# Gate and up projections: three of eight weight tiles with seven products, their shared sums written into the accumulators first

## The chip, the cores and the metric

The kernel runs on one core of a Trainium2 chip. The metric is the device time of one execution in microseconds (us). The work is shared by TensorE (PE, matrix products), ScalarE (ACT, copies and activations), VectorE (DVE, elementwise work), GpSimd (POOL, hardly used here) and SyncE (SP), which issues the loads from HBM. Each engine works off its own list of instructions in the order written in that list; an instruction whose input isn't ready, or whose output buffer isn't free yet, holds up everything behind it on its engine.

## The reference

One layer of a hybrid encoder on 256 positions with model width 2048: a projection of the normalised input, three mixers, an output projection, and a SwiGLU block. The change lies in the first half of the SwiGLU block alone:

```
h = rmsnorm(x, ffn_norm_g)                         # 256 x 2048
x = x + (silu(h @ w_gate) * (h @ w_up)) @ w_down   # w_gate, w_up: 2048 x 5632
```

All data are float32. The kernel keeps that accuracy by splitting every operand of a product into a high part (rounded to the narrower format fp32r) and the low rest, and summing three products: high x high, high x low, low x high. So each 128x128x512 block product costs three matmuls, and each weight needs two passes before it can be used: ACT writes the high part (`copy`), then DVE subtracts it from the weight (`subtract`) to get the low part.

## The kernel before

The 5632 columns of gate and up are worked off in 11 groups of 512 columns (`for g in range(11)`, L926). In a group the 2048 rows of the weights are 8 tiles of 256 rows (two blocks of 128), each loaded for gate and for up. A tile of gate and up together with the two blocks of 128 positions is a 2x2 by 2x2 block product, eight block products in all.

**Plain tiles** (`plain_unit`, L899). The eight block products go into four accumulators, PSUM banks of the pool `psA` (4 banks): c11 and c21 are gate for the first and second 128 positions, c12 and c22 are up. Per tile 4 x 2 x 3 = 24 matmuls, and two weight slabs of 128x1024, each with one ACT copy and one DVE subtraction (`halve`, L859). The four buffers for high parts and four for low parts go round.

**Fast tiles** (`fast_weights`, L866; `fast_unit`, L889). For the first `FAST = 2` tiles of a group the 2x2 by 2x2 product is done with seven block products in place of eight (Winograd's form of Strassen's scheme): 21 matmuls. It needs sums of the activations, which are made once (`turn_x2`, L805, into two packed tiles per weight tile), and differences of the weights, T, made for every group on DVE. Four of the products are shared between outputs and are summed in the four banks of the other PSUM pool, `psM` (ACROSS: p1, p6, p7, p5); three belong to one output each (ALONE: c11, c21, c12) and go straight into its accumulator. The differences have high and low parts of their own, in the buffers hT and lT, two of each, one per fast tile.

At the end of the shared products p1 is copied out of its bank by ACT (u1), and DVE makes u2 = p1 + p6, u3 = u2 + p7, u2 + p5 and u3 + p5 (L938 to L942), all held in SBUF. After the last plain tile DVE adds them to the four accumulators, ACT applies Silu, DVE multiplies gate with up (L951 to L955), and TensorE transposes the result (`turn_hid`, L912) among the plain tiles of the next group, into a `psM` bank too.

The order of each engine's list is made by a scheduler that goes through the program and takes, at each step, the instruction of highest priority that is ready by its estimates. Work inside `tc.high_priority(offset=ahead[0])` (loads and splitting of weights) is placed as though it stood 400 instructions earlier.

Of the kernel before, what the change touches and what calls it, by code (L numbers as in the profile page):

```python
# [30 lines left out]
ROWS = {"w_in": 2048, "w_uq": 512, "w_ukv": 256, "w_o": 2048, "w_gate": 2048, "w_up": 2048, "w_down": 5632}  # L31
# [21 lines left out]
SABBUFS = 3  # L53
WARM = 9
RAWS = 4
FAST = 2
MAGIC = 12582912.0
LOGEXP = "natural_log_exp_and_others"

# [1 line left out]
def build(tc, x, xT, pos, gains, fgain, lbraw, w_in, w_uq, w_ukv, w_o, w_gate, w_up, w_down, cst, msk, out, dbg=None):  # L61
    nc = tc.nc
    pe, act, dve, pool, sp = nc.tensor, nc.scalar, nc.vector, nc.gpsimd, nc.sync
# [41 lines left out]
    ahead = [0]  # L105
# [224 lines left out]
    f = rt(0)  # L330
# [464 lines left out]
    def wo_end(a, g):  # L795
        t = x2[g]
        for b in range(2):
            tt(t[:, b, :], t[:, b, :], a[b], ALU.add)
            junk = ffp.tile([P, 512], F32, name=nm("s1"), tag="s1", bufs=1)
            act.activation(junk, t[:, b, :], AF.Square, accum_out=ss2[:, 2 * g + b:2 * g + b + 1])  # L800
        kept = dram.tile([P, 2, 512], F32, name=nm("kept"), tag=f"kept{g}", bufs=1)
        act.dma_start(kept, t)
        x2kept.append(kept)

        def turn_x2():  # L805
            yield
            for i in range(2):
                n = 2 * g + i
                ps = transpose4([[t[:, b, (2 * i + j) * P:(2 * i + j + 1) * P] for b in range(2)] for j in range(2)])
                if n >= FAST:  # L810
                    at = act_tile()
                    for j in range(2):
                        split_act(at, j, ps[:, j * 256:(j + 1) * 256], gc(G_FFN, 2 * n + j))
                    x2T[n] = at
                    continue

                A = ffp.tile([P, 8, P], F32, name=nm("T"), tag="T")
                for j in range(2):
# [12 lines left out]
        spawn(turn_x2())
# [27 lines left out]
    def halve(src, js, hi=None, lo=None):  # L859
        hi = hi or slabp.tile([P, 2, 512], F32R, name=nm("hi"), tag="hi")  # L860
        lo = lo or slabp.tile([P, 2, 512], F32R, name=nm("lo"), tag="lo")
        act.copy(hi[:, js, :], src[:, js, :])  # L862
        tt(lo[:, js, :], src[:, js, :], hi[:, js, :].bitcast(F32), ALU.subtract)
        return hi, lo

    def fast_weights(wa, wb, r0, c0):  # L866

        with tc.high_priority(offset=ahead[0]):
            W = ffp.tile([P, 4, 512], F32, name=nm("W"), tag="W")
            for w, js in ((wb, slice(0, 2)), (wa, slice(2, 4))):  # L870
                at = ROWS[w.tensor.name] * c0 + r0 * 512
                sp.dma_start(W[:, js, :], w[at:at + 2 * P * 512].rearrange("(p t c) -> p t c", p=P, t=2))
            T = ffp.tile([P, 4, 512], F32, name=nm("T"), tag="T")
            tt(T[:, 0:2, :], W[:, 0:1, :].broadcast_to([P, 2, 512]), W[:, 1:3, :], ALU.subtract)
            tt(T[:, 2, :], W[:, 1, :], T[:, 1, :], ALU.subtract)
            tt(T[:, 3, :], W[:, 3, :], T[:, 2, :], ALU.subtract)
            hT = ffp.tile([P, 4, 512], F32R, name=nm("hT"), tag="hT")
            lT = ffp.tile([P, 4, 512], F32R, name=nm("lT"), tag="lT")
            a = halve(W[:, 2:4, :], slice(0, 2))
            halve(T, slice(0, 2), hT, lT)  # L880
            halve(T, slice(2, 4), hT, lT)
            b = halve(W[:, 0:2, :], slice(1, 2))
        return a, b, (hT, lT)


    ACROSS = (("p1", 0, 0, 0), ("p6", 5, 2, 2), ("p7", 6, 2, 0), ("p5", 4, 2, 1))
    ALONE = (("c11", 2, 0, 1), ("c21", 3, 2, 3), ("c12", 7, 1, 1))

    def fast_unit(accs, products, ws, forms, start):  # L889
        ah, al = forms  # L890
        for name, f, which, k in products:
            hi, lo = ws[which]
            o = accs[name]
            last = name[0] == "p" and start == "last"
            pe.matmul(o, lhsT=ah[:, f, :], rhs=hi[:, k, :], start=start is True, stop=False)  # L895
            pe.matmul(o, lhsT=ah[:, f, :], rhs=lo[:, k, :], start=False, stop=False)  # L896
            pe.matmul(o, lhsT=al[:, f, :], rhs=hi[:, k, :], start=False, stop=last)  # L897

    def plain_unit(accs, wa, wb, at, start, stop):  # L899
        for nme, b, (hi, lo) in (("c11", 0, wa), ("c21", 1, wa), ("c12", 0, wb), ("c22", 1, wb)):  # L900
            o = accs[nme]
            for j in range(2):
                ah = at[:, 0, j, b * P:(b + 1) * P]
                al = at[:, 1, j, b * P:(b + 1) * P]
                pe.matmul(o, lhsT=ah, rhs=hi[:, j, :], start=start and nme == "c22" and j == 0, stop=False)  # L905
                pe.matmul(o, lhsT=ah, rhs=lo[:, j, :], start=False, stop=False)  # L906
                pe.matmul(o, lhsT=al, rhs=hi[:, j, :], start=False, stop=stop and j == 1)  # L907

    def part(tag, bufs=1):
        return ffp.tile([P, 512], F32, name=nm(tag), tag=tag, bufs=bufs)  # L910
# [15 lines left out]
    for g in range(11):  # L926
        accs = {}
        fast = [fast_weights(w_gate, w_up, i * 256, g * 512) for i in range(FAST)]
        for n in ("p1", "p6", "p7", "p5"):
            accs[n] = bank()  # L930
        for i in range(FAST):
            fast_unit(accs, ACROSS, fast[i], x2T[i], True if i == 0 else "last" if i == FAST - 1 else False)
        for n in ("c11", "c21", "c12", "c22"):
            accs[n] = acc1()
        for i in range(FAST):
            fast_unit(accs, ALONE, fast[i], x2T[i], i == 0)
        u1, u3, u2, u4 = part("s1"), part("u3"), part("u2", 2), part("v", 2)
        act.copy(u1, accs["p1"])  # L938
        tt(u2, u1, accs["p6"], ALU.add)
        tt(u3, u2, accs["p7"], ALU.add)  # L940
        tt(u2, u2, accs["p5"], ALU.add)
        tt(u4, u3, accs["p5"], ALU.add)  # L942
        for i in range(FAST, 8):
            with tc.high_priority(offset=ahead[0]):
                wa = halve(load(w_gate, i * 256, g * 512), slice(0, 2))
                wb = halve(load(w_up, i * 256, g * 512), slice(0, 2))
            plain_unit(accs, wa, wb, x2T[i], i == FAST, i == 7)
            if g == 0 and i == FAST:
                flush()
            tick()  # L950
        for b, (ug, cg, uu, cu) in enumerate(((u1, "c11", u2, "c12"), (u3, "c21", u4, "c22"))):  # L951
            tt(ug, ug, accs[cg], ALU.add)
            act.activation(ug, ug, AF.Silu, scale=r2[:, b:b + 1])
            tt(uu, uu, accs[cu], ALU.add)
            stt(uu, uu, r2[:, b:b + 1], ug, ALU.mult, ALU.mult)  # L955
        spawn(turn_hid(g, (u2, u4)))

    hid = {}
    pairs = []
# [138 lines left out]
```

## Time and profile before

| | |
|---|---|
| median of 3 runs | 1132.84 us (1132.2 to 1132.9) |
| the profiled execution's own time | 1133.12 us |
| its span, first to last instruction | 1131.4 us |
| busy of the span: PE, DVE, ACT | 99%, 67%, 53% |
| granted TensorE clock over the span | 0.998 |
| gate and up, first matmul to the last group | 404 to about 880 us |
| one group in the steady state | 43.28 us, DVE busy for 33.40, ACT for 22.25 |

The busy share of an engine tells how much of the time something was in flight on it. The period of a group is read from the start of a group's first shared matmul to that of the next. A wait in the trace stands behind the instruction that waited, in brackets, with the engine and line that released it.

### The profile page before, as it was taken

The page shows a single profiled execution, that of the slowest core. Times are in us where ns is not written, and L with a number is a line of the kernel's source. Part 1 is how long each engine was busy: PE and PEld are TensorE (multiplying, and loading weights), DVE is VectorE, ACT ScalarE, POOL GpSimd, SP SyncE. Part 2 cuts the span into 40 slices and gives each one's busy share as a digit, 9 for nine tenths or more (in the row PEclk, how much of TensorE's full clock was granted, in tenths as well). Part 3 has the DMA queues.
Part 4 walks back from the last instruction along what each step waited for, and adds up shares of the span by engine and source line. Part 5 has one row for each costly group of instructions (what it writes and reads, how often), then busy time and mean ns, then how long its engine had stood idle before and what let it go on. Part 6 is the DMA issues. An engine that isn't in the chain of part 4 may idle for free.

```text
span 1131.4 us, 14321 instructions
## 1 busy us (share of the span) xinstructions
PE 1117.2 (99%) x5363; PEld 941.7 (83%) x5363; DVE 758.4 (67%) x907; ACT 595.2 (53%) x791; POOL 76.4 (7%) x110
## 2 busy tenths in 40 slices
PE   8999999999999999999999999999999999999997
PEld 5888899999988888888888888888888888888886
DVE  7798555455557876886886877876967645454543
ACT  7665565556545654554554555544546534443433
POOL 3196000010100000000000000000000000000000
PEclk9999999999999999999999999999999999999999
DMA  7745465544676765655656656556638666666662
GB/s 263 244 147 167 119 181 180 155 131 144 208 252 205 222 207 185 205 191 184 208 191 194 203 171 213 196 169 206 201 117 287 212 198 191 188 193 195 189 198 98
DMA packets 73302, 215.18 MB, mean 190 GB/s; under 512 B 7440, under 2 KB 24592, under 8 KB 73232
## 3 DMA queue, kind: packets, MB, share of 16 engines
q1 hardware_dynamic: 72656, 212.16, 58.8%
q10 hardware_dynamic: 576, 2.10, 0.5%
q8 instruction: 42, 0.69, 0.2%
q14 instruction: 28, 0.23, 0.1%
HBM read 210.04 MB, written 4.19 MB: 189 GB/s over the span
## 4 chain that ended last, share of the span: by engine, by line
PE 93%; DMA 2%; DVE 2%; issue 2%; ACT 1%; SPq 0%; POOL 0%; ACTq 0%; POOLq 0%; DVEq 0%
PE acc L153 15%; PE acc L155 15%; PE acc L154 15%; PE acc L906 10%; PE acc L907 10%; PE acc L905 10%; PE bank L248 2%; PE bank L895 2%; PE bank L896 2%; PE bank L897 2%; PE acc L895 1%; PE acc L896 1%; PE acc L897 1%; DVE lo L93 1%; PE bank L712 1%
## 5 line engine op out<-in xcount | busy, mean ns | idle before, releaser
L93 DVE TENSOR_TENSOR lo<-raw,hi 128x1024 fp32r<-128x1024 f32 (+3 forms) x366 | 424.3, 1167 | 279.3 <-ACT hi L121 217.7
L121 ACT CAST hi<-raw 128x1024 fp32r<-128x1024 f32 (+3 forms) x234 | 223.0, 956 | 246.2 <-PE acc L155 224.2
L154 PE MATMUL acc<-lo,at 128*128 128x512 f32 (+2 forms) x808 | 302.4, 374 | 3.1 <-DVE lo L93 2.9
L153 PE MATMUL acc<-hi,at 128*128 128x512 f32 (+2 forms) x808 | 304.4, 379 | 0.0
L155 PE MATMUL acc<-hi,at 128*128 128x512 f32 (+2 forms) x808 | 301.3, 373 | 0.0
L905 PE MATMUL acc<-hi,at 128*128 128x512 f32 x528 | 207.5, 393 | 0.0
L906 PE MATMUL acc<-lo,at 128*128 128x512 f32 x528 | 205.6, 389 | 0.3 <-DVE lo L93 0.3
L907 PE MATMUL acc<-hi,at 128*128 128x512 f32 x528 | 205.7, 390 | 0.0
L862 ACT CAST hi<-raw 128x1024 fp32r<-128x1024 f32 x132 | 136.6, 1051 | 130.0 <-PE acc L907 97.2
L154 PEld LDWEIGHTS acc<-lo,at 128*128 128x128 f32 x808 | 152.0, 188 | 29.3 <-DVE lo L93 7.6
L153 PEld LDWEIGHTS acc<-hi,at 128*128 128x128 f32 x808 | 151.7, 188 | 24.0 <-ACT hi L121 1.3
L155 PEld LDWEIGHTS acc<-hi,at 128*128 128x128 f32 x808 | 151.9, 188 | 22.1
L906 PEld LDWEIGHTS acc<-lo,at 128*128 128x128 f32 x528 | 99.2, 188 | 21.0 <-DVE lo L93 1.1
L907 PEld LDWEIGHTS acc<-hi,at 128*128 128x128 f32 x528 | 99.1, 188 | 20.8
L905 PEld LDWEIGHTS acc<-hi,at 128*128 128x128 f32 x528 | 99.2, 188 | 19.8
L177 POOL TENSOR_TENSOR sm<-sm,expo 128x4 f32<-128x4 f32 (+2 forms) x14 | 12.0, 858 | 896.8 <-DVE sm L102 896.8
L93 DVE TENSOR_TENSOR lo<-W,hi 128x1024 fp32r<-128x1024 f32 (+1 forms) x44 | 42.0, 956 | 34.6 <-ACT hi L862 34.6
L862 ACT CAST hi<-W 128x1024 fp32r<-128x1024 f32 (+1 forms) x44 | 36.7, 834 | 49.8 <-PE acc L907 42.7
L93 DVE TENSOR_TENSOR lT<-T,hT 128x1024 fp32r<-128x1024 f32 x44 | 52.6, 1216 | 0.0
L862 ACT CAST hT<-T 128x1024 fp32r<-128x1024 f32 x44 | 45.1, 1046 | 0.5 <-DVE T L93 0.4
L93 DVE TENSOR_TENSOR T<-W,T 128x512 f32<-128x512 f32 x44 | 30.0, 683 | 0.1
L93 DVE TENSOR_TENSOR T<-W 128x1024 f32<-128x1024 f32 x22 | 26.8, 1220 | 1.8 <-DMA W<-w_gate 1.6
(252 smaller groups left out, 1096.2 us busy)
## 6 DMA issues: line engine op xcount, KB each, us to landing
raw<-w_down SPq DMA_DIRECT2D x88, 512.0 KB, 4.2
raw<-w_gate SPq DMA_DIRECT2D x66, 512.0 KB, 4.1
raw<-w_up SPq DMA_DIRECT2D x66, 512.0 KB, 4.4
raw<-w_in SPq DMA_DIRECT2D x48, 384.0 KB, 3.5
raw<-w_in SPq DMA_DIRECT2D x32, 512.0 KB, 3.5
raw<-w_o SPq DMA_DIRECT2D x32, 512.0 KB, 4.3
W<-w_up SPq DMA_DIRECT2D x22, 512.0 KB, 3.6
W<-w_gate SPq DMA_DIRECT2D x22, 512.0 KB, 4.6
```

Of the source, the lines that this page charges most:

```text
L93: dve.tensor_tensor(o, a, b, op=op)
L121: act.copy(hi[:, js, :n], raw[:, js, :n])
L153: pe.matmul(o, lhsT=ah, rhs=hi[:, j, cs], start=start and j == 0, stop=False)
L154: pe.matmul(o, lhsT=ah, rhs=lo[:, j, cs], start=False, stop=False)
L155: pe.matmul(o, lhsT=al, rhs=hi[:, j, cs], start=False, stop=stop and j == 1)
L862: act.copy(hi[:, js, :], src[:, js, :])
L895: pe.matmul(o, lhsT=ah[:, f, :], rhs=hi[:, k, :], start=start is True, stop=False)
L896: pe.matmul(o, lhsT=ah[:, f, :], rhs=lo[:, k, :], start=False, stop=False)
L897: pe.matmul(o, lhsT=al[:, f, :], rhs=hi[:, k, :], start=False, stop=last)
L905: pe.matmul(o, lhsT=ah, rhs=hi[:, j, :], start=start and nme == "c22" and j == 0, stop=False)
L906: pe.matmul(o, lhsT=ah, rhs=lo[:, j, :], start=False, stop=False)
L907: pe.matmul(o, lhsT=al, rhs=hi[:, j, :], start=False, stop=stop and j == 1)
```

## The change

`FAST` goes from 2 to 3: per group a third tile with 21 matmuls, and five plain tiles in place of six. The weight tiles W get 3 buffers (2 before), T gets one (2 before); hT and lT keep two each. `fast_weights` now makes only the split parts of the four shared products, all in hT and lT; the three parts for the products of one output are split later by `alone_weights`, for the third tile into the same hT and lT buffers. So a group writes four pairs (hT, lT) into two buffers, where it was two pairs.

The sums are no longer added at the end. ACT copies p1 into c11's bank, u3 into c21's bank, DVE writes u2 + p5 and u3 + p5 into c12's and c22's banks, and only then do the matmuls of these accumulators start, adding to what stands there (no matmul of them has the start flag). The four adds behind the last plain tile are gone.

```diff
-FAST = 2
+FAST = 3
...
     def fast_weights(wa, wb, r0, c0):
         with tc.high_priority(offset=ahead[0]):
-            W = ffp.tile([P, 4, 512], F32, name=nm("W"), tag="W")
-            for w, js in ((wb, slice(0, 2)), (wa, slice(2, 4))):
-                at = ROWS[w.tensor.name] * c0 + r0 * 512
-                sp.dma_start(W[:, js, :], w[at:at + 2 * P * 512].rearrange("(p t c) -> p t c", p=P, t=2))
-            T = ffp.tile([P, 4, 512], F32, name=nm("T"), tag="T")
-            tt(T[:, 0:2, :], W[:, 0:1, :].broadcast_to([P, 2, 512]), W[:, 1:3, :], ALU.subtract)
+            W = ffp.tile([P, 4, 512], F32, name=nm("W"), tag="W", bufs=3)
...
+            sp.dma_start(W[:, 0:2, :], vb)
+            sp.dma_start(W[:, 3, :], va[:, 0, :])
+            sp.dma_start(W[:, 2, :], va[:, 1, :])
+            T = ffp.tile([P, 3, 512], F32, name=nm("T"), tag="T", bufs=1)
+            tt(T[:, 0:2, :], W[:, 0:1, :].broadcast_to([P, 2, 512]), W[:, 1:4:2, :], ALU.subtract)
             tt(T[:, 2, :], W[:, 1, :], T[:, 1, :], ALU.subtract)
-            tt(T[:, 3, :], W[:, 3, :], T[:, 2, :], ALU.subtract)
-            hT = ffp.tile([P, 4, 512], F32R, name=nm("hT"), tag="hT")
-            lT = ffp.tile([P, 4, 512], F32R, name=nm("lT"), tag="lT")
-            a = halve(W[:, 2:4, :], slice(0, 2))
-            halve(T, slice(0, 2), hT, lT)
-            halve(T, slice(2, 4), hT, lT)
-            b = halve(W[:, 0:2, :], slice(1, 2))
-        return a, b, (hT, lT)
+            tt(W[:, 0, :], W[:, 2, :], T[:, 2, :], ALU.subtract)
+            hT, lT = wide("hT"), wide("lT")
+            split(hT[:, 0:3, :], lT[:, 0:3, :], T)
+            split(hT[:, 3, :], lT[:, 3, :], W[:, 3, :])
+        return W, (hT, lT)
...
+    def split(hi, lo, src):
+        act.copy(hi, src)
+        tt(lo, src, hi.bitcast(F32), ALU.subtract)
+
+    def alone_weights(W, last):
+        with tc.high_priority(offset=ahead[0]):
+            if last:
+                hT, lT = wide("hT"), wide("lT")
+                split(hT[:, 0:3, :], lT[:, 0:3, :], W[:, 0:3, :])
+                return [(hT[:, k, :], lT[:, k, :]) for k in range(3)]
+            h1, l1 = halve(W[:, 0:2, :], slice(0, 2))
+            h2, l2 = halve(W[:, 2:4, :], slice(0, 1))
+        return [(h1[:, 0, :], l1[:, 0, :]), (h1[:, 1, :], l1[:, 1, :]), (h2[:, 0, :], l2[:, 0, :])]
...
+        for n in ("p1", "p6", "p7", "p5"):
+            across(n, 0)
+        for i in range(1, FAST):
+            for n in ("p1", "p6", "p7"):
+                across(n, i)
+        for i in range(1, FAST):
+            across("p5", i)
+        rest = [alone_weights(fast[i][0], i == FAST - 1) for i in range(FAST)]
         for n in ("c11", "c21", "c12", "c22"):
             accs[n] = acc1()
-        for i in range(FAST):
-            fast_unit(accs, ALONE, fast[i], x2T[i], i == 0)
-        u1, u3, u2, u4 = part("s1"), part("u3"), part("u2", 2), part("v", 2)
+        u1, u2, u3 = part("s1"), part("u2"), part("u3")
         act.copy(u1, accs["p1"])
+        act.copy(accs["c11"], u1)
         tt(u2, u1, accs["p6"], ALU.add)
         tt(u3, u2, accs["p7"], ALU.add)
-        tt(u2, u2, accs["p5"], ALU.add)
-        tt(u4, u3, accs["p5"], ALU.add)
+        act.copy(accs["c21"], u3)
+        tt(accs["c12"], u2, accs["p5"], ALU.add)
+        tt(accs["c22"], u3, accs["p5"], ALU.add)
+        for n in ("c11", "c21", "c12"):
+            for i in range(FAST - 1):
+                alone(n, i, rest[i])
+        for n in ("c11", "c21", "c12"):
+            alone(n, FAST - 1, rest[FAST - 1])
...
-        for b, (ug, cg, uu, cu) in enumerate(((u1, "c11", u2, "c12"), (u3, "c21", u4, "c22"))):
-            tt(ug, ug, accs[cg], ALU.add)
-            act.activation(ug, ug, AF.Silu, scale=r2[:, b:b + 1])
-            tt(uu, uu, accs[cu], ALU.add)
-            stt(uu, uu, r2[:, b:b + 1], ug, ALU.mult, ALU.mult)
-        spawn(turn_hid(g, (u2, u4)))
+        hh = []
+        for b, (cg, cu) in enumerate((("c11", "c12"), ("c21", "c22"))):
+            sg, v = part("sg", 2), part("v", 2)
+            act.activation(sg, accs[cg], AF.Silu, scale=r2[:, b:b + 1])
+            stt(v, accs[cu], r2[:, b:b + 1], sg, ALU.mult, ALU.mult)
+            hh.append(v)
+        spawn(turn_hid(g, hh))
```

How the lists of the engines change is shown at three places, for a group in the middle. The names: u_1088 and u_1089 (u_1069 and u_1068 before) are u2 and u3, s_... is u1, banks 5292 to 5295 are p1, p6, p7, p5 of this group, 5636 to 5638 are p1, p6, p7 of the next group, 5472 takes transposes of the group before; acc_5352, acc_5353, acc_5354 and acc_5355 are c11, c21, c12 and c22.

The first place is DVE at the start of a group. Before, u2 and u3 stand behind the first tile's differences and ahead of all the rest:

```order
L93 TENSOR_TENSOR T_5561<-W_5558 128x1024
L96 SCALAR_TENSOR_TENSOR u_1002_4976<-u_1002_4976,sm_3859,s_1000_4974 128x512
L93 TENSOR_TENSOR T_5561<-W_5558,T_5561 128x512
L96 SCALAR_TENSOR_TENSOR v_4977<-v_4977,sm_3859,u_1001_4975 128x512
L93 TENSOR_TENSOR T_5561<-W_5558,T_5561 128x512
L93 TENSOR_TENSOR u_1069_5314<-s_1067_5312,bank_5263 128x512
L93 TENSOR_TENSOR u_1068_5313<-u_1069_5314,bank_5264 128x512
L93 TENSOR_TENSOR T_5582<-W_5579 128x1024
```

Now, in the list after the change, DVE has this behind the low parts of the third tile's shared products (lT_5287, whose last row is the first here):

```order
L93 TENSOR_TENSOR lT_5287<-W_5278,hT_5286 128x512
L93 TENSOR_TENSOR T_5598<-W_5594 128x1024
L93 TENSOR_TENSOR lT_5349<-W_5278,hT_5348 128x1536
L93 TENSOR_TENSOR T_5598<-W_5594,T_5598 128x512
L93 TENSOR_TENSOR lT_5603<-W_5594,hT_5602 128x512
L93 TENSOR_TENSOR W_5594<-W_5594,T_5598 128x512
L93 TENSOR_TENSOR lo_5396<-raw_5393,hi_5395 128x1024
L93 TENSOR_TENSOR lo_5402<-raw_5399,hi_5401 128x1024
L93 TENSOR_TENSOR lT_5603<-T_5598,hT_5602 128x1536
L93 TENSOR_TENSOR u_1088_5357<-s_1087_5356,bank_5293 128x512
L93 TENSOR_TENSOR T_5612<-W_5608 128x1024
L93 TENSOR_TENSOR u_1089_5358<-u_1088_5357,bank_5294 128x512
```

T_5598 and lT_5603 belong to the next group's first tile, T_5612 to its second, lo_5396 and lo_5402 to this group's first plain tile. u2 has moved from the sixth row to behind all of them.

The second place is PE behind the products of one output. Before, the last of these products was followed by the first plain tile at once:

```order
L895 MATMUL acc_4954<-hi_4920,at_3477 128x512
L896 MATMUL acc_4954<-lo_4921,at_3477 128x512
L897 MATMUL acc_4954<-hi_4920,at_3478 128x512
L905 MATMUL acc_4952<-hi_4985,at_3550 128x512
L906 MATMUL acc_4952<-lo_4986,at_3550 128x512
L907 MATMUL acc_4952<-hi_4985,at_3550 128x512
```

Now, after the change, PE has done the nine products of c11 and one plain matmul when it comes to this:

```order
L917 MATMUL acc_5352<-lo_5396,at_3566 128x512
L917 MATMUL acc_5352<-hi_5395,at_3566 128x512 x2
L917 MATMUL acc_5352<-lo_5396,at_3566 128x512
L917 MATMUL acc_5352<-hi_5395,at_3566 128x512
L908 MATMUL bank_5636<-hT_5602,at_3461 128x512
L908 MATMUL bank_5636<-lT_5603,at_3461 128x512
L908 MATMUL bank_5636<-hT_5602,at_3462 128x512
L908 MATMUL bank_5637<-hT_5602,at_3461 128x512
L908 MATMUL bank_5637<-lT_5603,at_3461 128x512
L908 MATMUL bank_5637<-hT_5602,at_3462 128x512
L908 MATMUL bank_5638<-hT_5602,at_3461 128x512
L908 MATMUL bank_5638<-lT_5603,at_3461 128x512
```

Three shared products of the next group's first tile (9 matmuls; its p5 stays behind the last plain tile) have moved in ahead of c21's products, which follow two rows on.

The third place is ACT around the copy of p1. Before, the copy stood alone between a high part for the second tile's c12 product and the first plain slab:

```order
L862 CAST hi_5258<-W_5241 128x512
L938 COPY s_1067_5312<-bank_5262 128x512
L862 CAST hi_5323<-raw_5321 128x1024
L862 CAST hT_5565<-T_5561 128x1024
L862 CAST hi_5329<-raw_5327 128x1024
```

Now three wide copies into the hT buffers come ahead of it:

```order
L862 CAST hi_5344<-W_5264 128x512
L888 CAST hT_5286<-T_5282 128x1536
L888 CAST hT_5286<-W_5278 128x512
L888 CAST hT_5348<-W_5278 128x1536
L963 COPY s_1087_5356<-bank_5292 128x512
L964 COPY acc_5352<-s_1087_5356 128x512
L888 CAST hT_5602<-W_5594 128x512
L931 COPY at_5429<-bank_5430 128x512
L862 CAST hi_5395<-raw_5393 128x1024
L862 CAST hi_5401<-raw_5399 128x1024
L888 CAST hT_5602<-T_5598 128x1536
```

hT_5286 is the third tile's shared part and takes the buffer that the first tile had; hT_5348 is the third tile's part for its own three products and takes the second tile's; hT_5602 is the next group's.

## Rows read from the trace of the kernel before

**Rows 1.** The page: busy us, share and instructions; the chain that ended last, by engine.

```profile
PE 1117.2 (99%) x5363; PEld 941.7 (83%) x5363; DVE 758.4 (67%) x907; ACT 595.2 (53%) x791; POOL 76.4 (7%) x110
...
PE 93%; DMA 2%; DVE 2%; issue 2%; ACT 1%; SPq 0%; POOL 0%; ACTq 0%; POOLq 0%; DVEq 0%
```

**Rows 2.** Stretch of one group: us, busy us per engine (instructions), PEclk, DMA share, GB/s.

```profile
534.37:577.65 43.28, 43.28 (x196) 35.70 (x194) 33.40 (x37) 22.25 (x25) 0.00 (x0) 1.00 0.60 196
```

**Rows 3.** The waits of PE: engine, line, releaser, us in total, times, longest.

```profile
PE acc L154 <- DVE lo L93: 2.9, 6, 0.8
```

**Rows 4.** PE in order of time: start us, us, line, out<-in.

```profile
578.33 0.40 PE L895 MATMUL bank<-hT,at 128*128 128x512 f32 x1
...
580.20 0.40 PE L897 MATMUL bank<-hT,at 128*128 128x512 f32 x1
...
580.89 0.39 PE L897 MATMUL bank<-hi,at 128*128 128x512 f32 x1
...
587.35 0.39 PE L905 MATMUL acc<-hi,at 128*128 128x512 f32 x1
...
592.57 0.39 PE L907 MATMUL acc<-hi,at 128*128 128x512 f32 x1
...
593.47 0.39 PE L906 MATMUL acc<-lo,at 128*128 128x512 f32 x1
```

**Rows 5.** DVE operations by shape, 404 to 885 us: busy us, mean ns, idle before.

```profile
L93 DVE TENSOR_TENSOR lo<-raw,hi 128x1024 fp32r<-128x1024 f32 x136 | 164.0, 1221 | 63.7 <-ACT hi L862 60.7 <-ACT hi L121 2.4
...
L93 DVE TENSOR_TENSOR T<-W,T 128x512 f32<-128x512 f32 x40 | 27.3, 683 | 0.1
...
L93 DVE TENSOR_TENSOR u<-s,bank 128x512 f32<-128x512 f32 x11 | 7.5, 679 | 1.7 <-PE bank L897 1.7
```

**Rows 6.** ACT operations by shape, 404 to 885 us.

```profile
L862 ACT CAST hi<-raw 128x1024 fp32r<-128x1024 f32 x132 | 136.6, 1051 | 130.0 <-PE acc L907 97.2 <-PE acc L897 21.6 <-DMA raw<-w_up 3.3
...
L862 ACT CAST hi<-W 128x512 fp32r<-128x512 f32 x21 | 13.0, 620 | 27.8 <-PE acc L907 26.1 <-PE acc L155 1.7
...
L938 ACT COPY s<-bank 128x512 f32<-128x512 f32 x11 | 6.5, 587 | 29.7 <-PE bank L897 29.7
```

**Rows 7.** DVE in order of time, 577 to 621 us.

```profile
577.41 0.68 DVE L93 TENSOR_TENSOR u<-u,acc 128x512 f32<-128x512 f32 x1
578.01 0.68 DVE L93 TENSOR_TENSOR v<-v,acc 128x512 f32<-128x512 f32 x1
...
582.87 0.68 DVE L93 TENSOR_TENSOR u<-s,bank 128x512 f32<-128x512 f32 x1
583.65 0.69 DVE L93 TENSOR_TENSOR u<-u,bank 128x512 f32<-128x512 f32 x1
...
587.14 3.49 DVE L93 TENSOR_TENSOR lo<-raw,hi 128x1024 fp32r<-128x1024 f32 x3
...
599.10 0.68 DVE L93 TENSOR_TENSOR u<-u,bank 128x512 f32<-128x512 f32 x1
600.03 1.23 DVE L93 TENSOR_TENSOR lo<-raw,hi 128x1024 fp32r<-128x1024 f32 x1 [0.25 <-ACT hi L862]
```

**Rows 8.** ACT in order of time, 577 to 621 us.

```profile
581.36 0.59 ACT L938 COPY s<-bank 128x512 f32<-128x512 f32 x1 [2.83 <-PE bank L897]
...
586.01 2.94 ACT L862 CAST hi<-raw 128x1024 fp32r<-128x1024 f32 x3
...
598.95 1.05 ACT L862 CAST hi<-raw 128x1024 fp32r<-128x1024 f32 x1 [1.67 <-PE acc L907]
```

**Rows 9.** What ACT waited for, whole span.

```profile
ACT hi L862 <- PE acc L907: 139.9, 95, 2.0
```

**Rows 10.** Stretches at the start and the end, columns as in rows 2.

```profile
10.00:15.00 5.00, 3.87 (x15) 2.56 (x16) 4.75 (x6) 5.00 (x12) 2.80 (x3) 1.00 1.06 400
1124.00:1128.00 4.00, 0.00 (x0) 0.00 (x0) 1.46 (x4) 1.52 (x4) 0.56 (x1) 0.80 0.44 161
```

**Rows 11.** DMA issues of the fast tiles: count, KB each, us to landing.

```profile
W<-w_gate SPq DMA_DIRECT2D x22, 512.0 KB, 4.6
```

More of the change, by code (lines that the diff above doesn't have):

```diff
@@ L815, in turn_x2 @@
                     continue
-                A = ffp.tile([P, 8, P], F32, name=nm("T"), tag="T")
+                A = ffp.tile([P, 8, P], F32, name=nm("T"), tag="T", bufs=1)
                 for j in range(2):
@@ L887, in build @@
-    ALONE = (("c11", 2, 0, 1), ("c21", 3, 2, 3), ("c12", 7, 1, 1))
-    def fast_unit(accs, products, ws, forms, start):
-        ah, al = forms
[L891 to L897, printed above, removed]
@@ L899, in plain_unit @@
-    def plain_unit(accs, wa, wb, at, start, stop):
+            W = ffp.tile([P, 4, 512], F32, name=nm("W"), tag="W", bufs=3)
+            at = ROWS[wa.tensor.name] * c0 + r0 * 512
+            va, vb = (w[at:at + 2 * P * 512].rearrange("(p t c) -> p t c", p=P, t=2) for w in (wa, wb))
+            sp.dma_start(W[:, 0:2, :], vb)
+            sp.dma_start(W[:, 3, :], va[:, 0, :])
+            sp.dma_start(W[:, 2, :], va[:, 1, :])
+            T = ffp.tile([P, 3, 512], F32, name=nm("T"), tag="T", bufs=1)
@@ new lines, in fast_weights, with wide @@
+            tt(T[:, 0:2, :], W[:, 0:1, :].broadcast_to([P, 2, 512]), W[:, 1:4:2, :], ALU.subtract)
+            tt(T[:, 2, :], W[:, 1, :], T[:, 1, :], ALU.subtract)
+            tt(W[:, 0, :], W[:, 2, :], T[:, 2, :], ALU.subtract)
[3 more added lines that the diff above has]
+        return W, (hT, lT)
+    def wide(tag):
+        return ffp.tile([P, 4, 512], F32R, name=nm(tag), tag=tag)
@@ L900, in plain_unit, with product @@
+    ACROSS = {"p1": (0, 3), "p6": (5, 2), "p7": (6, 0), "p5": (4, 1)}
+    ALONE = {"c11": (2, 2), "c21": (3, 0), "c12": (7, 1)}
+    def product(o, forms, f, hi, lo, start, stop):
+        ah, al = forms
+        for lhsT, rhs, k in ((ah, hi, 0), (ah, lo, 1), (al, hi, 2)):
+            pe.matmul(o, lhsT=lhsT[:, f, :], rhs=rhs, start=start and k == 0, stop=stop and k == 2, skip_group_check=True)
+    def plain_unit(accs, wa, wb, at, stop):
         for nme, b, (hi, lo) in (("c11", 0, wa), ("c21", 1, wa), ("c12", 0, wb), ("c22", 1, wb)):
@@ L904, in plain_unit @@
                 al = at[:, 1, j, b * P:(b + 1) * P]
-                pe.matmul(o, lhsT=ah, rhs=hi[:, j, :], start=start and nme == "c22" and j == 0, stop=False)
-                pe.matmul(o, lhsT=ah, rhs=lo[:, j, :], start=False, stop=False)
-                pe.matmul(o, lhsT=al, rhs=hi[:, j, :], start=False, stop=stop and j == 1)
+                for lhsT, rhs, k in ((ah, hi, 0), (ah, lo, 1), (al, hi, 2)):
+                    pe.matmul(o, lhsT=lhsT, rhs=rhs[:, j, :], start=False, stop=stop and j == 1 and k == 2, skip_group_check=True)
     def part(tag, bufs=1):
@@ L930, in build, with across, alone @@
             accs[n] = bank()
-        for i in range(FAST):
-            fast_unit(accs, ACROSS, fast[i], x2T[i], True if i == 0 else "last" if i == FAST - 1 else False)
+        def across(n, i):
+            f, k = ACROSS[n]
+            hT, lT = fast[i][1]
+            product(accs[n], x2T[i], f, hT[:, k, :], lT[:, k, :], i == 0, i == FAST - 1)
+        def alone(n, i, ws):
+            f, k = ALONE[n]
+            product(accs[n], x2T[i], f, *ws[k], False, False)
+        for n in ("p1", "p6", "p7", "p5"):
[6 more added lines that the diff above has]
+        rest = [alone_weights(fast[i][0], i == FAST - 1) for i in range(FAST)]
         for n in ("c11", "c21", "c12", "c22"):
             accs[n] = acc1()
-        for i in range(FAST):
-            fast_unit(accs, ALONE, fast[i], x2T[i], i == 0)
-        u1, u3, u2, u4 = part("s1"), part("u3"), part("u2", 2), part("v", 2)
+        u1, u2, u3 = part("s1"), part("u2"), part("u3")
         act.copy(u1, accs["p1"])
+        act.copy(accs["c11"], u1)
         tt(u2, u1, accs["p6"], ALU.add)
         tt(u3, u2, accs["p7"], ALU.add)
-        tt(u2, u2, accs["p5"], ALU.add)
-        tt(u4, u3, accs["p5"], ALU.add)
+        act.copy(accs["c21"], u3)
[6 more added lines that the diff above has]
+            alone(n, FAST - 1, rest[FAST - 1])
         for i in range(FAST, 8):
@@ L946, in build @@
                 wb = halve(load(w_up, i * 256, g * 512), slice(0, 2))
[L947 removed]
+            plain_unit(accs, wa, wb, x2T[i], i == 7)
             if g == 0 and i == FAST:
@@ L965, in split_hid @@
             if n % 2 == 0:
-                pairs.append(ffp.tile([P, 2, 2, 2, 256], F32R, name=nm("T"), tag="T"))
+                pairs.append(ffp.tile([P, 2, 2, 2, 256], F32R, name=nm("W"), tag="W", bufs=3))
             at = pairs[-1][:, n % 2]
```

1 line of the change is left out of this document (removed).

## Prediction

> **What bounds the kernel now.** I read the page first: PE is busy for 99% of the span and makes up 93% of the chain that ended last [rows 1]. Then the stretches cut at the groups of gate and up: a group takes 43.28 us, PE never idle in it, DVE busy for 33.40 and ACT for 22.25 [rows 2]. PE's waits in the whole span are a few us, the largest entry 2.9 us in six pieces, before the gate and up stage [rows 3]. So a matmul taken away here is worth its pitch, as long as nothing else comes to be waited for. The pitch follows from PE in order of time: 24 plain matmuls start at 587.35 to 592.57, 23 pitches of 0.227 us; those that read hT and lT start at 578.33 to 580.20, 8 pitches of about 0.233 [rows 4]. The last plain matmul before four transposes starts at 592.57, the second one after them at 593.47: 0.90 less two pitches leaves 0.45 for the four [rows 4].
>
> **What it removes.** Per group 24 plain matmuls become 21, and the number that read hT and lT goes from 24 to 45. Without waits a group would take 45 x 0.233 + 138 x 0.227 + 0.9 (eight transposes) = 42.7 us, 0.56 less than now, 6.2 us over the 11 groups. The four adds behind the last plain tile (4 x 0.68) leave DVE too, but PE does not wait for them now.
>
> **What it adds and moves.** The work of splitting and adding grows little (DVE from 33.4 to about 35 us in a group), but three things now stand in a row right at the start of a group. First, hT and lT have two buffers for four uses, so the third tile's shared pair can be written only when p5 of the first tile has read the buffer. Second, the accumulators can't start until p1's copy, u2 and u3 are there. Third, DVE's list puts u2 and u3 behind the next group's splitting. In the kernel before, u2 + p5 is added at 599.10, 15 us after u3 at 583.65, with its inputs long there [rows 7]: DVE takes its list in order, and then it cost nothing, since PE needed it only at the group's end.
>
> I walk through a group in the middle, 0 being the end of the last plain tile before it. Durations: DVE starts one 128x512 operation 0.60 us after the other (577.41, 578.01), 1024 wide 1.135 (three in 3.49 with 1.22 for the last) [rows 7]; 1536 wide isn't in the trace. Its bounds are one 1024-wide and two of them, 1.135 and 2.27; I take 1.67, on the line through 512 and 1024. An operation alone takes 0.68 and 1.22 [rows 5]. ACT: 0.62 and 1.05 alone [rows 6], 0.945 from start to start at 1024 (2.94 for three) [rows 8], so 0.52 at 512, and for 1536 1.37 from start to start, 1.48 alone. From PE to ACT 0.08 (580.89 + 0.39 to 581.36) [rows 4, 8], from ACT to DVE 0.03 (598.95 + 1.05 to 600.03) [rows 7, 8]; to PE I take 0.1, an estimate from these.
>
> PE does p5 of the first tile, 3 matmuls, to 0.70; the last has drained 0.16 later. ACT writes hT for the third tile from 0.94 to 2.42, the 512-wide piece to 2.93. DVE, free before, starts at 2.45: lT 1.67, lT 0.60, T of the next group 1.135, so 5.86. Then lT for the third tile's own products: its ACT copy had to wait for p5 of the second tile (drained at about 4.3) and ends at 5.88, so DVE goes on at 5.93 and is at 7.60. Then T, lT, W at 0.60 each: 9.40. Two plain low parts: 11.67. lT of the next group: 13.34. u2: 13.94. T of the next group's second tile: 15.08. u3 ends at 15.76.
>
> PE meanwhile: 9 matmuls of the second tile to 2.79; the third tile's and the rest, with waits of 0.24 for hT and lT, to 6.4; four transposes; c11 waits for p1's two copies on ACT (5.77 to 7.00, queued behind the wide copy) and runs from 7.1 to 9.15; one plain matmul after 0.06 of waiting, four transposes to 9.88; the plain low part of DVE is there at 10.62, so PE goes on at 10.72 and is through five more at 11.85. Then p1 of the next group (12.0, its bank behind an ACT copy). p6 needs the bank that u2 reads: 14.12, a wait of 1.4. p7 needs the one that u3 reads: 15.86, a wait of 1.1. c21 needs the copy of u3 (15.79 + 0.59 [rows 6] = 16.4) and finds it at 16.56. The other 36 matmuls to the end of the first plain tile run through to 24.77, as c12 and c22 are written by 18.2; without waits PE would be there at 20.92. So 3.85 us of waiting, and four plain tiles follow (96 x 0.227 = 21.8) in which DVE and ACT catch up: ACT already waits 95 times for PE to free a high-part buffer [rows 9]. The group takes 46.57 us, 3.3 more than before.
>
> **Other edits.** ACT's copy into a PSUM bank and DVE's sum into one aren't in the trace. Bounds: nothing to gain below the 0.52 at which ACT starts copies one after the other, and 1.05 for one of twice the width; I take 0.59, as for the copy out of a bank [rows 6]. On the path lies one ACT copy per group, so -0.1 to +0.5 us a group. The Trainium skill, Perfetto Trace Analysis, Optimizing Scalar/DVE Operations, has about 51 ns of overhead for ACT on PSUM and 93 on SBUF; by that the copy would be some 0.04 us cheaper, under 1 us in all. No run here shows it yet. The extra loads move the same bytes in smaller pieces. The next group's W is free once its own halves are split, some 4 us before 0, and lands in 4.6 [rows 11], while DVE comes to it at 4.7; without that cover DVE's row, and PE behind it, moves by as much as the load is late. The third packed activation tile adds about 1 us each to ACT and DVE in the stage before, beside PE's matmuls; I give it nothing, and 1 us if it shows.
>
> **The sum.** Nine groups in the middle: 9 x 3.3 = 29.7. The first group has none of its shared products done ahead and the products wait for the same row of DVE from a start 2 us later, with two small sums more: about 5.5 of waiting less 0.56, 4.9. The last has no next group's splitting ahead of u2: u3 ends at 9.5, c21 at 10.7 waits under 1 us, in all 1.5 less 0.56, 0.9. Together +35.5 on the profiled execution's 1133.1 (span 1131.4 and 1.7 around it, 0.3 above the median): 1168 us.
>
> **Rivals.** *The sums come in time.* Were u3 there before PE comes to p7 (11.8 without waits, in place of 15.76), only the matmuls would count: 1133.1 - 6.2 = 1127. For it: DVE is idle for 10 us of a group [rows 2]. Against it: the idle time lies late in a group, and nine operations stand ahead of u2. It needs DVE a third faster than in rows 5, or the wide pair 4 us sooner. 6%. With some 6 us of the 41 us of waits left, gain and loss cancel (1133): 4%.
>
> *PE loses its clock in the new gaps.* 4 us of waits in 25 recur in every group. At the start of the program PE is idle for 1.1 of 5 us and the granted clock stays 1.00; at the end, with PE idle throughout, it falls to 0.80 [rows 10]. If the fall came, one plain tile at half the clock would take 10.9 for 5.44 us: +54 over ten groups, 1222. From the first of these rows I hold it unlikely: 3%. The Trainium skill, TensorE: Matmul & The Clock Gate, Why this matters for your kernels, warns of idle gaps between bursts of matmuls; the trace agrees in the stretch at the end, not in the one at the start.
>
> **How the numbers follow.** The forecast, slower by DVE's row at the start of a group: 87%. Its own range: with 1536-wide operations at the bounds, three in the row, each group moves by -1.6 to +1.8, ten of them by -16 to +18: 1152 to 1186. I give 1150 to 1184; out of it lie the rivals and the forecast's edges. What can be told from no change is about 0.2%, 2.3 us: faster 0.07, same 0.03, slower 0.90.
>
> **What would show it.** The period of a group at about 46.6 us; DVE without a gap for the first 16 us of a group; PE waiting before the next group's second and third shared product for the sums on DVE (1.4 and 1.1 us), and for the first plain low part (0.8); no wait in the last four plain tiles; the clock at 1.0. A period under 43, or u2 starting less than 3 us after p1's copy, would make it wrong.

## The result, and the profile after

The changed kernel takes 1180.52 us (median of 6 runs, 1177.94 to 1184.4), the kernel before 1132.87 beside it: a ratio of 1.042, 95% interval 1.041 to 1.0431. That is 47.6 us more, where 35 were forecast. The profiled execution has a span of 1178.6 us, 47.2 above the span of before, and a mean granted clock of 0.987, before 0.998.

The page, its busy line and its chain, against [rows 1]:

```profile
PE 1136.4 (96%) x5330; PEld 939.8 (80%) x5330; DVE 775.9 (66%) x910; ACT 624.2 (53%) x825; POOL 76.6 (6%) x110
...
PE 83%; DVE 10%; issue 3%; ACT 2%; DMA 1%; POOL 0%; SPq 0%; ACTq 0%; POOLq 0%; DVEq 0%
```

PE issues 33 matmuls less, three in each of 11 groups, and is busy for 19 us more: in part because some of them ran slowly. DVE has gone from 2 to 10% of the chain, though its share of busy time is lower than before. Next, stretches of the changed kernel (us, busy us of PE, PEld, DVE, ACT and POOL with instructions, PEclk, DMA share, GB/s): the second of the eleven groups, two later groups, which answer to [rows 2], and 20 us of each of these two with the waits in them:

```profile
455.83:503.88 48.05, 45.54 (x199) 35.80 (x198) 35.31 (x37) 24.93 (x28) 0.00 (x0) 1.00 0.54 176
...
552.09:598.75 46.66, 44.13 (x192) 34.68 (x191) 34.94 (x37) 24.93 (x28) 0.00 (x0) 1.00 0.57 181
598.75:646.98 48.23, 45.73 (x192) 35.87 (x191) 34.95 (x37) 24.91 (x28) 0.00 (x0) 0.96 0.55 175
...
560.00:580.00 20.00, 17.47 (x76) 13.28 (x75) 18.02 (x20) 10.72 (x13) 0.00 (x0) 1.00 0.56 175
600.00:620.00 20.00, 17.50 (x69) 12.54 (x68) 16.20 (x18) 10.46 (x13) 0.00 (x0) 0.91 0.47 157
```

The two later groups stand for two kinds. Both hold the same 192 matmuls and both leave PE idle for 2.5 us. One takes 46.66 us at a clock of 1.00; in the other part of the work runs at the lower level, 1.2 GHz, and it takes 48.23. Of the nine groups between the first and the last, two are of the first kind (46.66, 46.64) and six of the second (48.15 to 48.23). The ninth, the second of the eleven, takes 48.05 us for another reason: its clock stays at 1.00, but it holds six shared matmuls more, as the first group takes only three of its matmuls ahead and not nine (6 x 0.233 = 1.4 us).

What PE waits for (engine, line, releaser, us in total, times, longest us); of the four rows only the third was there before [rows 3]:

```profile
PE bank L908 <- DVE u L93: 18.1, 19, 1.2
PE acc L917 <- DVE lo L93: 6.3, 10, 1.0
PE acc L154 <- DVE lo L93: 2.9, 6, 0.8
PE bank L248 <- DVE u L93: 2.1, 1, 2.1
```

PE in order of time (start us, us, line, out<-in, in brackets the idle time before and its releaser) in the two later groups (the first row is of an earlier one), to be laid beside [rows 4]:

```profile
519.70 0.80 PE L908 MATMUL bank<-hT,at 128*128 128x512 f32 x1 [0.77 <-DVE u L93]
...
566.18 0.50 PE L908 MATMUL bank<-hT,at 128*128 128x512 f32 x1 [1.17 <-DVE u L93]
...
567.91 0.50 PE L908 MATMUL bank<-hT,at 128*128 128x512 f32 x1 [0.77 <-DVE u L93]
...
568.72 0.40 PE L908 MATMUL acc<-hi,at 128*128 128x512 f32 x1
568.95 0.39 PE L908 MATMUL acc<-lo,at 128*128 128x512 f32 x1
...
598.75 0.40 PE L908 MATMUL bank<-hT,at 128*128 128x512 f32 x1
...
609.45 0.50 PE L917 MATMUL acc<-lo,at 128*128 128x512 f32 x1 [0.57 <-DVE lo L93]
...
612.85 0.50 PE L908 MATMUL bank<-hT,at 128*128 128x512 f32 x1 [1.16 <-DVE u L93]
...
614.58 0.50 PE L908 MATMUL bank<-hT,at 128*128 128x512 f32 x1 [0.76 <-DVE u L93]
...
615.46 0.63 PE L908 MATMUL acc<-hi,at 128*128 128x512 f32 x1
615.89 0.63 PE L908 MATMUL acc<-lo,at 128*128 128x512 f32 x1
...
619.27 0.40 PE L908 MATMUL acc<-lo,at 128*128 128x512 f32 x1
```

598.75 is the forecast's point 0 of the slower of the two. The waits in front of the next group's p6 and p7 (1.16 and 0.76) and of the first plain low part (0.57) are the same in both groups to 0.02 us. Behind them c21 goes at 0.23 us a matmul in the faster group (568.72 to 568.95) and at 0.43 in the slower (615.46 to 615.89), until it is back at 0.23 some 3.4 us later. That costs the 1.56 us between the two kinds. The fall isn't tied to an instruction: in an earlier group (the first row above) it comes with the first matmul of p7.

DVE in order of time in the slower group, to be laid beside [rows 7]:

```profile
601.17 1.76 DVE L93 TENSOR_TENSOR lT<-T,hT 128x1536 fp32r<-128x1536 f32 x1 [0.71 <-ACT hT L888]
602.85 0.68 DVE L93 TENSOR_TENSOR lT<-W,hT 128x512 fp32r<-128x512 f32 x1
...
604.69 1.76 DVE L93 TENSOR_TENSOR lT<-W,hT 128x1536 fp32r<-128x1536 f32 x1
...
612.11 0.68 DVE L93 TENSOR_TENSOR u<-s,bank 128x512 f32<-128x512 f32 x1
...
613.85 0.68 DVE L93 TENSOR_TENSOR u<-u,bank 128x512 f32<-128x512 f32 x1
...
620.32 2.36 DVE L93 TENSOR_TENSOR lo<-raw,hi 128x1024 fp32r<-128x1024 f32 x2 [3.38 <-ACT hi L862]
```

From 601.17 to 616.9 DVE has no gap; then it is idle for 3.4 us. u2 (L93, out of the copy and p6's bank) starts at 612.11, though the last shared product had been started on PE by 604.94. The operations that the trace of before didn't have, by shape (busy us, mean ns, idle before), beside [rows 5, 6]:

```profile
L93 DVE TENSOR_TENSOR lT<-T,hT 128x1536 fp32r<-128x1536 f32 x33 | 58.0, 1756 | 12.5 <-ACT hT L888 12.5
...
L93 DVE TENSOR_TENSOR acc<-u,bank 128x512 f32<-128x512 f32 x22 | 15.1, 688 | 0.0
```

```profile
L888 ACT CAST hT<-T 128x1536 fp32r<-128x1536 f32 x33 | 48.8, 1479 | 4.5 <-PE bank L908 3.0
...
L964 ACT COPY acc<-s 128x512 f32<-128x512 f32 x11 | 6.5, 591 | 0.3
...
L963 ACT COPY s<-bank 128x512 f32<-128x512 f32 x11 | 6.3, 574 | 0.0
```

ACT still waits for PE to free high-part buffers, less often than in [rows 9]; and the loads of a fast tile land in about the time they took before [rows 11]:

```profile
ACT hi L862 <- PE acc L917: 118.7, 82, 1.7
```

```profile
W<-w_up SPq DMA_DIRECT2D x33, 512.0 KB, 3.9
W<-w_gate SPq DMA_DIRECT2D x66, 256.0 KB, 4.3
```

### The profile page after: what moved, and what is told of

Read it like the earlier page. It is cut to its first block, busy times and chain, and to the rows that moved or that the text cites. A ratio compares the mean times of both kernels' runs of the same rounds, so it can differ in the third digit from the quotient of the medians.

```text
span 1178.6 us, 14304 instructions
## 1 busy us (share of the span) xinstructions
PE 1136.4 (96%) x5330; PEld 939.8 (80%) x5330; DVE 775.9 (66%) x910; ACT 624.2 (53%) x825; POOL 76.6 (6%) x110
## 4 chain that ended last, share of the span: by engine, by line
PE 83%; DVE 10%; issue 3%; ACT 2%; DMA 1%; POOL 0%; SPq 0%; ACTq 0%; POOLq 0%; DVEq 0%
PE acc L917 24%; PE acc L153 15%; PE acc L154 15%; PE acc L155 14%; PE acc L908 5%; PE bank L908 4%; DVE lT L93 4%; DVE lo L93 2%; DVE T L93 2%; ACT hT L888 1%; PE bank L248 1%; DVE u L93 1%; PE bank L712 1%; PE bank L411 1%; DMA raw<-w_in 0%
## 5 line engine op out<-in xcount | busy, mean ns | idle before, releaser
L93 DVE TENSOR_TENSOR lo<-raw,hi 128x1024 fp32r<-128x1024 f32 (+3 forms) x344 | 397.8, 1164 | 287.6 <-ACT hi L121 218.1
L917 PE MATMUL acc<-hi,at 128*128 128x512 f32 x880 | 275.1, 390 | 0.0
L917 PEld LDWEIGHTS acc<-hi,at 128*128 128x128 f32 x880 | 165.2, 188 | 35.9 <-ACT hi L862 2.1
L917 PE MATMUL acc<-lo,at 128*128 128x512 f32 x440 | 172.5, 392 | 6.3 <-DVE lo L93 6.3
L862 ACT CAST hi<-raw 128x1024 fp32r<-128x1024 f32 x110 | 113.7, 1053 | 116.8 <-PE acc L917 69.0
L153 PEld LDWEIGHTS acc<-hi,at 128*128 128x128 f32 x808 | 151.6, 188 | 25.3 <-ACT hi L121 2.5
L155 PEld LDWEIGHTS acc<-hi,at 128*128 128x128 f32 x808 | 151.7, 188 | 22.2
L908 PE MATMUL bank<-hT,at 128*128 128x512 f32 x264 | 93.2, 417 | 18.1 <-DVE u L93 18.1
L908 PEld LDWEIGHTS bank<-hT,at 128*128 128x128 f32 x264 | 49.7, 192 | 39.9 <-DVE u L93 26.3
L93 DVE TENSOR_TENSOR lo<-W,hi 128x1024 fp32r<-128x1024 f32 (+1 forms) x44 | 42.1, 956 | 50.0 <-ACT hi L862 50.0
L93 DVE TENSOR_TENSOR lT<-T,hT 128x1536 fp32r<-128x1536 f32 x33 | 58.0, 1756 | 12.5 <-ACT hT L888 12.5
L908 PE MATMUL acc<-hi,at 128*128 128x512 f32 x132 | 52.4, 453 | 0.6 <-ACT acc L967 0.6
L908 PE MATMUL bank<-lT,at 128*128 128x512 f32 x132 | 52.7, 413 | 0.0
L888 ACT CAST hT<-T 128x1536 fp32r<-128x1536 f32 x33 | 48.8, 1479 | 4.5 <-PE bank L908 3.0
```

Of the source, the lines that this page charges most:

```text
L153: pe.matmul(o, lhsT=ah, rhs=hi[:, j, cs], start=start and j == 0, stop=False)
L155: pe.matmul(o, lhsT=al, rhs=hi[:, j, cs], start=False, stop=stop and j == 1)
L888: act.copy(hi, src)
L908: pe.matmul(o, lhsT=lhsT[:, f, :], rhs=rhs, start=start and k == 0, stop=stop and k == 2, skip_group_check=True)
L917: pe.matmul(o, lhsT=lhsT, rhs=rhs[:, j, :], start=False, stop=stop and j == 1 and k == 2, skip_group_check=True)
```

## Experiments

All times stand against the kernel before, run beside them on the same chip (1133.77 us beside the first four kernels, 1132.93 beside the last two). Theory: PE loses its time to the order on DVE, where u2 and u3 stand behind other work, and the half clock follows from the gaps this makes. Rivals: two buffers of hT and lT for four uses; the writes into the accumulators themselves; a clock that falls for reasons of its own.

**Useless matmuls in the gaps.** In the loop that issues the first tile's shared products, from the second group on:

```diff
         for n in ("p1", "p6", "p7", "p5"):
+            f, k = ACROSS[n]
+            for _ in range({"p1": 5, "p6": 3}.get(n, 0) if g else 0):
+                pe.matmul(accs[n], lhsT=x2T[0][0][:, f, :], rhs=fast[0][1][0][:, k, :], start=True, stop=True, ...)
             across(n, 0)
```

> The changed kernel with eight useless matmuls a group from the second group on: five into the bank of the next group's first shared product (p1) and three into that of the second (p6), each ahead of the first matmul of that product, which starts the bank anew, so the values stay the same. They stand where PE waits 1.16 us for u2 and 0.76 us for u3. Theory 'the row on DVE, and the clock with it': the sums come when they came, so the eight matmuls (1.9 us) fall into time in which PE stood idle; if the half clock of about 3.4 us after these gaps, seen in eight of ten groups, comes from the gaps, it goes, and every group takes the 46.65 us of the two groups that kept the clock: some 8 x 1.57 = 12.6 us less than the changed kernel, 1168 us (1164 to 1172), granted clock 0.998 in the page. Rival 'the clock falls for the work, not the gaps' (or by itself): the fall stays, 1180 or more, mean clock 0.987 or less. Rival 'the matmuls are simply added': 10 x 1.9 = +19 us, 1199.

Measured: 1172.4 us (1171.67 to 1175.81), ratio 1.0351, interval 1.0333 to 1.0369; 8 us less than the changed kernel, with 80 matmuls more, and no run of the one reaches into the range of the other. PE around the start of one group (L954 are the useless ones), and the 20 us around it:

```profile
612.60 0.50 PE L917 MATMUL acc<-lo,at 128*128 128x512 f32 x1 [0.58 <-DVE lo L93]
613.89 1.43 PE L954 MATMUL bank<-hT,at 128*128 128x512 f32 x5
616.00 0.96 PE L954 MATMUL bank<-hT,at 128*128 128x512 f32 x3
```

```profile
600.00:620.00 20.00, 19.35 (x84) 14.15 (x83) 18.79 (x21) 11.69 (x15) 0.00 (x0) 1.00 0.59 201
```

Eight of the nine groups in the middle now take 46.65 us each, at a clock of 1.00. So the fall comes from the two gaps in front of p6 and p7, filled together here, and not from PE's work: the wait for the plain low part (0.58) got no useless matmuls and is still there, at a clock of 1.00. The row on DVE alone makes 46.65. The expected 12.6 us became 8, and 1172.4 us is 0.4 above the expected range, because the expectation counted eight falls. The changed kernel has six in these eight groups, and they went (382.6 us to 373.2); the first group, whose own gaps got no useless matmuls, lost its clock as before; and the second, which had no fall to lose, takes 49.87 us for 48.05, as it holds 16 matmuls more, of which 8 fall into gaps.

**The sums first on DVE.** The same instructions; only their priority is changed:

```diff
-        act.copy(u1, accs["p1"])
-        ...
-        tt(accs["c22"], u3, accs["p5"], ALU.add)
+        with tc.high_priority(offset=2 * ahead[0]):
+            act.copy(u1, accs["p1"])
+            ...
+            tt(accs["c22"], u3, accs["p5"], ALU.add)
```

> The changed kernel with the copies and sums of the shared products given a higher priority, so that on DVE u2 and u3 stand right behind the splitting of the third tile's own products and ahead of the next group's, and the next group's shared products are no longer pulled ahead on PE. Theory 'the row on DVE': by the same durations as in the forecast u2 ends at 8.2 and u3 at 9.4 us after the end of the last plain tile (13.9 and 15.8 before), c21's copy at 10.1 where PE comes at about 9.6; of the 3.85 us of waits some 0.8 are left, a period of 43.0 to 44.2, the clock keeps 1.00, and the whole takes 1137 us (1130 to 1146). Rival 'two buffers of hT and lT for four uses': these waits are as before, period over 46, 1165 or more. Rival 'writing into the accumulators': the copies and sums into PSUM hold the products of one output wherever they stand, period 45 to 46, 1150 to 1160.

Measured: 1138.16 us, ratio 1.0046, interval 1.0031 to 1.0061, a period of 43.71 us. Its waits of PE in the stage, then one group and DVE in it (point 0 at 579.32):

```profile
PE acc L908 <- ACT acc L968: 3.2, 11, 0.6
```

```profile
535.60:579.32 43.72, 43.45 (x193) 34.88 (x192) 35.10 (x37) 24.91 (x28) 0.00 (x0) 1.00 0.62 193
```

```profile
588.79 0.68 DVE L93 TENSOR_TENSOR u<-s,bank 128x512 f32<-128x512 f32 x1
589.39 0.68 DVE L93 TENSOR_TENSOR T<-W,T 128x512 f32<-128x512 f32 x1
589.99 0.68 DVE L93 TENSOR_TENSOR u<-u,bank 128x512 f32<-128x512 f32 x1
```

DVE does the same work in a group (35.1 us, in the changed kernel 34.9), with the same two buffers of hT and lT and the same writes, and 42 of the 47.6 us are gone; the mean clock is back at 0.998. What cost them was the order. The priority moved PE's list too, since the next group's products are no longer taken ahead, so this run doesn't part DVE's order from PE's. But taking these products off PE's list would not by itself have brought c21 forward in the changed kernel, as it starts at 615.46, right behind ACT's copy of u3:

```profile
614.56 0.59 ACT L967 COPY acc<-u 128x512 f32<-128x512 f32 x1 [3.89 <-DVE u L93]
```

u2 ended at 10.2, not at 8.2 as expected: without the next group's products pulled ahead, PE reads the first tile's hT later, and DVE starts later. PE comes to c21 later for the same reason, so only 0.3 us a group is left of the waits, on ACT's copy of u3.

**Two tiles, sums into the accumulators.**

```diff
-FAST = 3
+FAST = 2
```

> One half of the change: two tiles with seven products as before, but the sums written into the accumulators, to which the rest then adds, and the code of the change otherwise (FAST = 2). Theory 'the row on DVE': with two tiles the splitting for the group's own products is shorter and u2, u3 follow it directly, so u3 is there at about 6 us, ahead of PE, which comes to c21 at about 8.4; little is lost against the kernel before, 1136 us (1131 to 1142). Rival 'writing into the accumulators costs by itself': a wait of about 3 us a group stays, 1160 to 1175.

Measured: 1137.4 us, ratio 1.0038, interval 1.0023 to 1.0053, period 43.57, PE busy for all of it. With two tiles, writing into the accumulators, together with the rest of the changed code, costs 0.3 us a group, not 3, and no wait in the groups in the middle. Where the 0.3 lies isn't shown.

**Three tiles, sums at the end.** The matmuls start the accumulators themselves again (the start flags are left out of the cut below).

```diff
-        act.copy(accs["c11"], u1)
         tt(u2, u1, accs["p6"], ALU.add)
         tt(u3, u2, accs["p7"], ALU.add)
-        act.copy(accs["c21"], u3)
-        tt(accs["c12"], u2, accs["p5"], ALU.add)
-        tt(accs["c22"], u3, accs["p5"], ALU.add)
+        tt(u2, u2, accs["p5"], ALU.add)
+        tt(u4, u3, accs["p5"], ALU.add)
...
+            tt(ug, ug, accs[cg], ALU.add)
+            tt(uu, uu, accs[cu], ALU.add)
```

> The other half of the change: three tiles with seven products, but the sums kept in SBUF and added behind the last plain tile as in the kernel before; the products of one output and c22 start their accumulators themselves. Theory 'the row on DVE holds PE only through the sums': PE then waits for nothing but hT and lT (about 0.3 us a group), the period is 42.9 to 43.3, and the whole 1130 us (1126 to 1136), a little under the kernel before. Rival 'the third tile itself is too much for DVE and ACT at the start of a group (two buffers for four uses)': period over 45, 1155 or more.

Measured: 1128.59 us, ratio 0.9954, interval 0.9937 to 0.997: 0.5% less than the kernel before. One group, then the sums on DVE in the next (point 0 at 579.0):

```profile
536.17:579.02 42.85, 42.85 (x192) 34.97 (x191) 37.24 (x41) 23.83 (x26) 0.00 (x0) 1.00 0.60 196
```

```profile
600.23 0.68 DVE L93 TENSOR_TENSOR u<-s,bank 128x512 f32<-128x512 f32 x1
...
608.25 0.67 DVE L93 TENSOR_TENSOR u<-u,bank 128x512 f32<-128x512 f32 x1
```

DVE has 2.3 us more to do than in the changed kernel, and u2 starts at 21 us, u3 at 29, far later than there (13.4 and 15.1). PE waits for neither, since no matmul of the group needs them. Against the two-tile form of before, the third tile gives 43.28 - 42.85 = 0.43 us a group.

**The same again, and with four tiles.** The first is the last kernel unchanged, timed once more; the second has FAST = 4 in it.

> The kernel with three tiles and the sums at the end once more, in more rounds and beside the one with four tiles, for its interval against the kernel before. Theory: period 42.85 us against 43.28 in ten or eleven groups, 4.3 to 4.7 us less than before, 1128 to 1129 us, ratio 0.996. Rival 'a chance of three rounds': within 0.2% of before.

> As the run with three tiles and the sums at the end, but with four of the eight tiles made of seven products (FAST = 4). 24 matmuls of 0.227 us become 21 and 21 more go to the 0.233 pitch: 0.56 us a group less if PE waits for nothing, 42.3 us a group and 1122 to 1125 us in all. Theory 'what stands in a row at the start of a group decides': the fourth tile's hT and lT can be written only when p5 of the second tile has been read, so on DVE lT of the third tile, the fourth tile's T, lT and W and its lT (some 7 us from the first ACT copy at 2.4) end at 9 to 10 us, where PE needs them at about 8.6; the tile's own low parts follow. A wait of 0.5 to 2 us a group comes back, period 42.8 to 44.3, 1128 to 1145 us, the clock at 1.00 if the gaps are like those of the sums-first run. Rival 'there is room': no wait, 1122 to 1126. Rival 'the row breaks': waits of over 3 us and the half clock with them, 1160 or more.

Measured: three tiles 1128.41 us, ratio 0.9957, interval 0.9944 to 0.997, as before. Four tiles 1126.06 us (1124.76 to 1130.24), ratio 0.9942, interval 0.9929 to 0.9954, period 42.31 against 42.88 for three. The wait that I expected didn't come: the rival, that there is room, was right. On PE, products of single outputs of earlier tiles stand among the shared ones of the fourth; that this is what covers its late pair is likely, but no run tests it. One group:

```profile
534.32:576.62 42.30, 42.30 (x190) 34.41 (x189) 41.29 (x46) 25.13 (x28) 0.00 (x0) 1.00 0.60 203
```

DVE is now busy for 41.3 of 42.3 us, so a fifth tile would hardly find room (not tried). The groups give 9.0 us from the first shared product to the last plain matmul (477.0 before, 468.1 now); the profiled spans differ by 7.2, so 1.8 are lost in the stages around, which I didn't look into.

## Why the prediction was right, and where it was not

*The row on DVE.* Right in place and size. Forecast from 598.75 on: the first wide lT at 2.45, the wide lT of the tile's own products at 5.93, u2 done at 13.94, u3 at 15.76, PE going on with p6 at 14.12 and with p7 at 15.86. The rows show 2.42, 5.94, 14.04, 15.78, 14.10 and 15.83. The period without a fall of the clock is 46.65, forecast 46.57, and PE waits for nothing in the last four plain tiles. The two estimated durations held: behind a 1536-wide operation DVE starts the next 1.68 us later (601.17 to 602.85; 1.67 was assumed), and ACT's copy takes 1.48 us, as assumed. That it is the order that costs, and not the amount of work, the buffers or the writes, was only argued; the sums-first, two-tile and sums-at-end runs show it.

*The removed matmuls.* Right: with no wait left a group takes 42.85, calculated 42.7.

*The clock.* Here the forecast failed: "the clock at 1.0" held in three groups of nine. The rival "PE loses its clock in the new gaps" stood at 3% and as something that comes in place of the forecast, at 5.4 us a group. It came on top, at 1.56 us in six of nine groups. I had held it unlikely from one stretch at the program's start, in which PE was idle for 1.1 of 5 us and kept its clock [rows 10]; the two kinds of group above, alike in PE's gaps and unlike in clock, show that one such stretch proves nothing. The Trainium skill, TensorE: Matmul & The Clock Gate, A second HAM failure mode: psum-queue depth-cycling, tells of a kernel whose short, frequent waits between groups of matmuls over PSUM banks made the clock go up and down. The trace agrees, with waits of 0.6 to 1.2 us, most of them for banks; this section, and not the one weighed in the prediction, was the one that bears on the change.

*The sum.* In the profiled executions, from the end of one group's last plain matmul to the next (the first group from its first shared matmul on):

| stretch | forecast | measured | of it half clock |
|---|---|---|---|
| first group | +4.9 | +7.5 (51.2 for 43.7) | at most 3.4 |
| nine in the middle | +29.7 | +40.5 (430.6 for 390.1) | 6 x 1.56 = 9.4 |
| last group | +0.9 | -1.2 (42.1 for 43.3) | 0 |
| sum | +35.5 | +46.8 | at most 12.8 |

The first group's 3.4 us are from the clock of two stretches:

```profile
420.00:425.00 5.00, 3.24 (x9) 0.57 0.43 149
425.00:430.00 5.00, 5.00 (x18) 0.74 0.00 0
```

(columns: PE alone, PEclk, DMA share, GB/s; 5 us x 0.43 and 5 us x 0.26, less where PE stood idle at the lower level.) Without the clock the sum is at least +34.0.

The forecast also left out where nine shared matmuls fall. A group in the middle hands nine to the group before and takes nine of the next. The first group hands on none and takes three (0.7 us more), so the second holds six more (1.4) and the last nine fewer (2.1); over all groups this comes to nothing. With it the middle is met: 40.5 - 9.4 - 1.4 = 29.7. The last group is 2.1 under the forecast. Its wait did come, for the copy of u3 in front of c21, at 0.60 us, where under 1 was forecast:

```profile
897.25 0.50 PE L908 MATMUL acc<-hi,at 128*128 128x512 f32 x1 [0.60 <-ACT acc L967]
```

The first group's waits sum to 3.75 us (51.02 long, PE busy for 47.27), where about 5.5 were forecast.

*What was luck.* The 1180.5 us lie in the forecast's 1150 to 1184, but that range was drawn for the unmeasured 1536-wide operations, which came out as assumed. The room above was used up by the clock, for which the range had no term.

*Small terms.* The copy into an accumulator takes 591 ns, the assumed 0.59; the copy out of a bank to SBUF 574. By the figures of the Trainium skill, Perfetto Trace Analysis, Optimizing Scalar/DVE Operations, as the prediction read them, the first would be an estimated 0.04 us cheaper; the rows show it 0.02 dearer. The loads moved in smaller pieces land in 3.9 and 4.3 us [rows 11: 4.6] and held up nothing.

## What to carry to other kernels

A wait that moves from the end of a stage to its start is paid for with what stands ahead of it in the list of the engine that ends it: walk that list with measured durations before the edit, and then either bring the awaited operations forward (42 us here) or keep the engine that bounds from needing them until late (52 us here). Where the bounding engine is TensorE, add to each row of short recurring waits a price for the clock, as a term of the sum and not as a rival to it (here 1.56 us a fall, in two groups of three). An engine with idle time in the mean has room only where nobody waits for its order; with the sums at the end even a fourth tile fitted.

## What was not expected of the hardware

- Useless matmuls in PE's waits made the kernel faster: 80 more, 8 us less, since the clock stayed at 1.00 in all later groups.
- The same waits (1.16 and 0.76 us, to 0.02) cost the clock in six of the nine groups in the middle and not in three, and the fall came at different instructions. The timed runs of the changed kernel go with their mean clock: 1177.94 us at 0.989, 1184.4 at 0.985. What decides whether a group keeps its clock stays open.
